# Head outputs turned on VectorE in 32x32 blocks, the blocks moved by DMA, and tokens kept in the turned order

## The chip, the cores and the metric

The kernel runs on one core of one Trainium2 chip. The metric is the device time of the core in microseconds. A core has TensorE (PE in the profile; its weight loads are PEld), VectorE (DVE), ScalarE (ACT), GpSimd (POOL) and SyncE (SP), each with an instruction queue of its own that runs in order. SP, ACT and POOL also issue DMAs.

## The reference

One encoder layer: 512 tokens, width 1024, all in float32. Two mixers work on the same normed input, their results are gated and summed, and a SwiGLU block follows.

```python
h = RMSNorm(x)
xc, gb, gc, q, k, v, g_sw, gate_a, gate_r = split(h @ W_in)

u    = gc * xc
conv = u[t-1] * w0 + u[t] * w1 + u[t+1] * w2
y_a  = (gb * conv) @ w_a_out

ret = retention(rotary(q), rotary(k), v)          # 4 heads, decayed in both directions
ret = (ret - mean(ret)) * rsqrt(var(ret) + eps) * g_ret     # per head and token
y_r = (ret * silu(g_sw)) @ w_r_out

x = x + (sigmoid(gate_a) * y_a + sigmoid(gate_r) * y_r) @ w_o
x = x + (silu(RMSNorm(x) @ w_gate) * (RMSNorm(x) @ w_up)) @ w_down
return RMSNorm(x)
```

A head has 256 query and key features and 512 value features.

## The kernel before

Every float32 product is made of three float32r matmuls (`mm3`): a number is split into a rounded part (hi) and the rest (lo), and hi x hi, hi x lo and lo x hi are added in PSUM. `split` makes the pair: ScalarE casts or scales the source into hi (L208, or L211 with a scale), VectorE subtracts it and stores lo (L209, or L212 with a scale). Many products use Strassen's scheme on quarters; the sums of weights which that needs are made on VectorE (L307).

Weights come from DRAM in units of 512 KB: SP loads a unit into one of ten raw tiles (L246 for plain blocks, L292 for quarters), and `split` makes its hi and lo tiles, of which there are five pairs. Large activations live in 14 "big" tiles of [128, 4, 512].

The part around the change runs over the four heads h. For each, `load_head` brings the scaled queries and keys, decay tables, values and swish gates from DRAM on SP (L879, L884). `do_pv` multiplies the scores with the values: four token tiles nb of 128 tokens, tokens on partitions and 512 features on the free axis; the mean and variance follow (L918 to L921), VectorE subtracts the mean and multiplies the gate (L927), ScalarE multiplies the reciprocal deviation (L929). The result lies in the gates' tile. The next head's scores follow (`do_scores`, `split_v`).

The projection `do_wr` needs the head output with features on partitions, so `do_t` turns it: `transpose` issues 16 VectorE instructions (L224), one for each pair (b, q) of a band of 32 partitions b and a quarter q of the features. Each reads 32 partitions x 512 elements in 32x32 blocks and writes them to band q of the target, so that tokens stand in natural order. Then four scaled splits (the gain `g_ret`) make the pair `yr`. `do_wr(h - 1)` runs next, while `do_t(h)` works: two halves of the 1024 output columns, each with 48 matmuls into four PSUM banks (`token_major`), then four evictions, which copy (L959) or add (L961) into `ysum`; with the last head they are also multiplied by the R gates `sgr` (L963). With head 0 the last convolution block `do_mix(3)` takes the place of `do_wr`. After the last head `do_wr(3)` runs directly behind `do_wr(2)`.

The convolution runs feature-major: `mix_quads` and `do_mix` make it in a tile c, multiply by the branch B in place (L870, L843), and `z_forms` splits the product and its Strassen sums and stores them to DRAM. `load_z` brings them back on POOL (L945), and the Strassen product that starts behind `do_wr(3)` reads them; its evictions (`merge`) multiply by the A gates `sga` and add `ysum`. After the output projection and the second norm the normed rows are transposed on TensorE. Until there the tokens of a tile nb are 128 nb + p on partition p.

In SwiGLU the same turning is done by `gated` (two transposes of 128x256 for a token tile, L1233) and `scatter` (16 DMAs on SP, L1243), which leave the tokens in another order: tile b, then j, then r for token 128 j + 32 b + r. The running sum is stored to DRAM in that order (L1335 to L1338), and the host puts the rows back at the end (L1529).

Tiles are placed and the instructions of each queue are put in order by a scheduler, mostly in the order of the program; `tc.issue_after(i)` puts the instructions of a block behind i on its engine.

Of the kernel before, what the change touches and what calls it, by code (L numbers as in the profile page):

```python
# [12 lines left out]
F32 = mybir.dt.float32  # L13
F32R = mybir.dt.float32r
AF = mybir.ActivationFunctionType
ALU = mybir.AluOpType

P = 128
D = 1024
S = 512  # L20
KD = D // P
NB = S // P
HEADS = 4
# [152 lines left out]
def block_kernel(ctx: ExitStack, tc: tile.TileContext, xw0, xw, xT, xtok, wpack, wquad, cols, decs, rot, g_ffn, g_final, out):  # L176
    nc = tc.nc
# [14 lines left out]
    def bigtile(dt=F32, n=4):  # L192
        return big.tile([P, n, 512], dt, tag="big", name="big", padded_shape=[P, 4, 512])
# [8 lines left out]
    low_of = [None]  # L202
    hi_of = [None]

    def split(src, hi, lo, scale=None, round=None):

        if scale is None:
            first = (round or nc.scalar.copy)(hi, src)  # L208
            low_of[0] = nc.vector.tensor_tensor(out=lo, in0=src, in1=hi.bitcast(F32), op=ALU.subtract)  # L209
        else:  # L210
            first = nc.scalar.activation(hi, src, AF.Copy, scale=scale)  # L211
            nc.vector.scalar_tensor_tensor(  # L212
                out=lo, in0=src, scalar=scale, in1=hi.bitcast(F32),
                op0=ALU.mult, op1=ALU.subtract)
        hi_of[0] = first
        return first

    def transpose(out, src):

        for b in range(4):  # L220
            for q in range(4):
                i = src[32 * b:32 * b + 32].rearrange("p j (i q c) -> p j i q c", q=4, c=32)
                o = out[32 * q:32 * q + 32].rearrange("p i (j b c) -> p j i b c", b=4, c=32)
                nc.vector.transpose(o[:, :, :, b, :], i[:, :, :, q, :])  # L224


    pos = [0]
    block = [0]
# [129 lines left out]
    def mm3(ps, left, right, first, last):  # L358
        (lh, ll), (rh, rl) = left, right
        nc.tensor.matmul(ps, lh, rh, start=first, stop=False)  # L360
        nc.tensor.matmul(ps, lh, rl, start=False, stop=False)  # L361
        nc.tensor.matmul(ps, ll, rh, start=False, stop=last)  # L362

    def act_pair(tiles, k, sl=slice(0, S)):
        hi, lo = tiles
        return hi[k // 4][:, k % 4, sl], lo[k // 4][:, k % 4, sl]
# [7 lines left out]
                mm3(ps, c.w(k, m * P, P), act_pair(rhs, k), k == 0, k == 7)  # L374
            evict(block0 + m, ps)

    def token_major(lhs, row0, chunks, evict, before=None):


        pss = [bank() for _ in range(NB)]  # L380
        n = 4 * chunks
        for kk in range(n):
            if kk % 4 == 0:
                c = Chunk()
            if before:
                before(kk)
            for nb in range(NB):
                mm3(pss[nb], act_pair(lhs, row0 + kk, slice(nb * P, (nb + 1) * P)),
                    c.w(kk % 4, 0, 512), kk == 0, kk == n - 1)
        for nb in range(NB):  # L390
            evict(nb, pss[nb])

# [117 lines left out]
    gret = cols_sb[:, O_GRET:O_GRET + 16]  # L510
# [134 lines left out]
    grd = [kept(f"gr{j}") for j in range(2)]  # L645
# [16 lines left out]
    for h in range(EARLY):  # L662
        pss = [bank() for _ in range(4)]
        for kk in range(8):
            if kk % 4 == 0:
                c = Chunk()
# [23 lines left out]
        t = bigtile()  # L690
# [138 lines left out]
        put(2, w)  # L829
        put(3, x2[:, 1:2])  # L830

    def do_mix(s):
        us, c = [], bigtile()[:, 0:2, :]
        feature_major(xg, lambda m, ps: us.append(snap(ps)))
        u = u_tile()

        def ev_c(m, ps):
            nc.vector.tensor_tensor(out=u[:, m, 1:513], in0=ps, in1=us[m], op=ALU.mult)
            conv(m, 2 * s + m, u[:, m], c[:, m])
        feature_major(xg, ev_c)  # L840

        def ev_b(m, ps):
            nc.vector.tensor_tensor(out=c[:, m], in0=ps, in1=c[:, m], op=ALU.mult)  # L843
        feature_major(xg, ev_b)
        z_forms(s, c)

    T1, T2 = slice(0, 256), slice(256, 512)

    def halves(t):
        return t.rearrange("p (m t) -> p m t", m=2)  # L850

    def mix_quads():

        c = bigtile().rearrange("p (s m) t -> p s m t", s=2)
        for s in range(2):
            u, got = u_tile(), {}

            def ev21(ps):
                nc.vector.tensor_tensor(out=u[:, :, 257:513], in0=halves(ps), in1=halves(got["c2"]), op=ALU.mult)

            def ev12(t):
                nc.vector.tensor_tensor(out=u[:, :, 1:257], in0=halves(got["x1"]), in1=halves(t), op=ALU.mult)
            fm_quad(xf, lambda t: got.update(x1=t), ev21, lambda t: got.update(c2=t), ev12)
            for m in range(2):
                conv(m, 2 * s + m, u[:, m], c[:, s, m])

        def times(s, t):
            def ev(b):
                o = c[:, s, :, t]
                nc.vector.tensor_tensor(out=o, in0=halves(b), in1=o, op=ALU.mult)  # L870
            return ev
        fm_quad(xf, times(0, T1), times(0, T2), times(1, T2), times(1, T1))
        for s in range(2):
            z_forms(s, c[:, s])


    def load(src, dt=F32):
        t = bigtile(dt)
        nc.sync.dma_start(t if dt == F32 else t.bitcast(F32), src)  # L879
        return t  # L880

    def load_head(h):
        tab = misctile(896, "tab")
        nc.sync.dma_start(tab, tabs[h])  # L884
        return [load(t, F32R) for t in qkd[h]], tab, load(vd[h]), load(sgd[h])

    def do_scores(qk, tab):
        p = (bigtile(F32R), bigtile(F32R))
# [40 lines left out]
            nc.scalar.activation(t, t, AF.Copy, scale=mv[:, 3:4])  # L929

    def do_t(h, t):
        tt = bigtile()
        transpose(tt, t)
        yr = (bigtile(F32R), bigtile(F32R))
        for eb in range(4):
            split(tt[:, eb, :], yr[0][:, eb, :], yr[1][:, eb, :], gret[:, 4 * h + eb:4 * h + eb + 1])
        return [yr[0]], [yr[1]]

    def load_z(groups):
        for j in groups:  # L940
# [7 lines left out]

    ysum, zf = [], {}

    def do_wr(h, yr):

        if h == 0:
            ysum.extend([bigtile(), bigtile()])
        for half in range(2):
            def ev(nb, ps):
                t = ysum[half][:, nb, :]
                if h == 0:
                    nc.scalar.copy(t, ps)  # L959
                else:  # L960
                    nc.vector.tensor_tensor(out=t, in0=ps, in1=t, op=ALU.add)  # L961
                if h == HEADS - 1:
                    nc.vector.tensor_tensor(out=t, in0=t, in1=sgr[half][:, nb, :], op=ALU.mult)  # L963
            token_major(yr, 0, 1, ev)

    mix_quads()
    nxt = load_head(0)
# [3 lines left out]
    yr = None  # L971
    for h in range(HEADS):
        if h < HEADS - 1:
            nxt = load_head(h + 1)
        else:
            load_z((0,))
        do_pv(p, vv, sg)
        t = sg
        if h < HEADS - 1:
            p = do_scores(nxt[0], nxt[1])  # L980
            vv, sg = split_v(nxt[2]), nxt[3]
        else:
            load_z((1, 2))
        new = do_t(h, t)
        if h == 0:
            do_mix(3)
        else:
            if h == HEADS - 1:
                sgr = [load(t) for t in grd]
            do_wr(h - 1, yr)  # L990
        yr = new


    load_z((3,))
    sga = [bigtile(), bigtile()]
    for t, d in zip(sga, gad):
        nc.gpsimd.dma_start(t, d)
    do_wr(HEADS - 1, yr)

    def merge(half, o):  # L1000
# [529 lines left out]
```

## Time and profile before

| | us |
|---|---|
| median of 3 runs | 1015.35 |
| lowest, highest | 1015.1, 1016.31 |
| the profiled execution | 1016.66 |
| its span | 1014.4 |
| PE busy in it | 1002.5 |
| DVE busy | 894.2 |
| ACT busy | 547.4 |
| POOL busy | 154.3 |
| mean granted clock of TensorE | 0.996 of full |

Times in the views are microseconds from the start of the span; where the page gives ns for one instruction, that is the mean. Matmuls overlap: one takes 0.39 us in the records, while the next starts after about 0.23. A line number names the line that issued the instruction, often a helper's. "x16" is the number of instructions in a row or group; what stands behind "<-" in brackets is the work that ended the idle time before it.

### The profile page before, as it was taken

The page shows a single profiled execution, that of the slowest core. Times are in us where ns is not written, and L with a number is a line of the kernel's source. Part 1 is how long each engine was busy: PE and PEld are TensorE (multiplying, and loading weights), DVE is VectorE, ACT ScalarE, POOL GpSimd, SP SyncE. Part 2 cuts the span into 40 slices and gives each one's busy share as a digit, 9 for nine tenths or more (in the row PEclk, how much of TensorE's full clock was granted, in tenths as well). Part 3 has the DMA queues.
Part 4 walks back from the last instruction along what each step waited for, and adds up shares of the span by engine and source line. Part 5 has one row for each costly group of instructions (what it writes and reads, how often), then busy time and mean ns, then how long its engine had stood idle before and what let it go on. Part 6 is the DMA issues. An engine that isn't in the chain of part 4 may idle for free.

```text
span 1014.4 us, 13342 instructions
## 1 busy us (share of the span) xinstructions
PE 1002.5 (99%) x4746; PEld 838.4 (83%) x4746; DVE 894.2 (88%) x1163; ACT 547.4 (54%) x736; POOL 154.3 (15%) x246
## 2 busy tenths in 40 slices
PE   9999999999999999999999999999999999999996
PEld 7888888888888998888888888888887888888884
DVE  7878898979798888697989997999988996989897
ACT  7547655553655455343452325577665555574664
POOL 0030221222122004112221200011101000003202
PEclk9999999999999999999999999999999999999998
DMA  9525587695767658839687865467677369486953
GB/s 352 189 76 184 185 289 219 206 306 177 231 191 257 222 217 276 332 131 331 154 306 257 288 233 180 127 202 231 167 228 152 139 208 267 107 248 127 274 140 104
DMA packets 60642, 215.87 MB, mean 213 GB/s; under 512 B 8928, under 2 KB 9056, under 8 KB 55968
## 3 DMA queue, kind: packets, MB, share of 16 engines
q1 hardware_dynamic: 42592, 144.73, 41.7%
q0 software_dynamic: 17696, 70.01, 25.6%
q8 instruction: 37, 0.61, 0.3%
q10 hardware_dynamic: 288, 0.29, 0.1%
q14 instruction: 29, 0.24, 0.1%
HBM read 171.21 MB, written 57.41 MB: 225 GB/s over the span
## 4 chain that ended last, share of the span: by engine, by line
PE 87%; DVE 8%; issue 2%; SPq 2%; DMA 1%; ACT 1%; POOL 0%; POOLq 0%; DVEq 0%; ACTq 0%
PE bank L445 48%; PE bank L360 10%; PE bank L361 10%; PE bank L362 10%; PE bank L401 8%; DVE wlo L209 2%; SPq L1243 2%; DVE raw L307 1%; DMA big<-turned 1%; DVE turned L1233 1%; DVE t L1229 1%; DVE t L1182 0%; DVE big L209 0%; PE bank L501 0%; ACT whi L208 0%
## 5 line engine op out<-in xcount | busy, mean ns | idle before, releaser
L208 ACT CAST whi<-raw 128x1024 fp32r<-128x1024 f32 (+2 forms) x299 | 301.8, 1028 | 239.0 <-PE bank L445 73.5
L209 DVE TENSOR_TENSOR wlo<-raw,whi 128x1024 fp32r<-128x1024 f32 (+2 forms) x300 | 350.8, 1189 | 69.6 <-ACT whi L208 68.9
L445 PE MATMUL bank<-whi,xform 128*128 128x512 f32 x1056 | 330.5, 390 | 0.0
L445 PEld LDWEIGHTS bank<-whi,xform 128*128 128x128 f32 x1056 | 198.0, 188 | 42.2 <-DVE xform L209 1.0
L445 PE MATMUL bank<-wlo,xform 128*128 128x512 f32 x528 | 205.8, 390 | 0.5 <-DVE wlo L209 0.5
L445 PE MATMUL bank<-whi,big 128*128 128x512 f32 x596 | 187.5, 390 | 0.3 <-ACT t L452 0.3
L307 DVE TENSOR_TENSOR raw<-raw 128x1024 f32<-128x1024 f32 x112 | 132.2, 1198 | 0.8
L445 PEld LDWEIGHTS bank<-whi,big 128*128 128x128 f32 x596 | 111.7, 188 | 24.5 <-ACT t L452 1.1
L445 PEld LDWEIGHTS bank<-wlo,xform 128*128 128x128 f32 x528 | 99.1, 188 | 22.1 <-DVE wlo L209 1.7
L445 PE MATMUL bank<-wlo,big 128*128 128x512 f32 x298 | 116.1, 390 | 0.1
L452 ACT COPY t<-bank 128x512 f32<-128x512 f32 x95 | 55.5, 587 | 70.8 <-PE bank L445 55.8
L360 PE MATMUL bank<-big,whi 128*128 128x512 f32 x220 | 85.7, 390 | 0.0
L362 PE MATMUL bank<-big,wlo 128*128 128x512 f32 x220 | 85.6, 389 | 0.0
L361 PE MATMUL bank<-big,whi 128*128 128x512 f32 x220 | 85.6, 389 | 0.0
L445 PEld LDWEIGHTS bank<-wlo,big 128*128 128x128 f32 x298 | 55.9, 188 | 12.0 <-DVE wlo L209 0.6
L401 PE MATMUL bank<-xform,whi 128*128 128x256 f32 x304 | 55.3, 283 | 0.2 <-ACT t L452 0.2
L360 PE MATMUL bank<-whi,big 128*128 128x512 f32 x128 | 49.8, 389 | 0.0
L361 PE MATMUL bank<-wlo,big 128*128 128x512 f32 x128 | 49.8, 389 | 0.0
L362 PE MATMUL bank<-whi,big 128*128 128x512 f32 x128 | 49.8, 389 | 0.0
L362 PEld LDWEIGHTS bank<-big,wlo 128*128 128x128 f32 x220 | 41.3, 188 | 8.7
L361 PEld LDWEIGHTS bank<-big,whi 128*128 128x128 f32 x220 | 41.3, 188 | 8.5
L360 PEld LDWEIGHTS bank<-big,whi 128*128 128x128 f32 x220 | 41.3, 188 | 8.5
(211 smaller groups left out, 1395.1 us busy)
## 6 DMA issues: line engine op xcount, KB each, us to landing
raw<-wquad SPq DMA_DIRECT2D x140, 512.0 KB, 5.2
raw<-wpack SPq DMA_DIRECT2D x42, 512.0 KB, 5.9
raw<-wquad POOLq DMA_DIRECT2D x16, 512.0 KB, 6.4
t_g<-wquad POOLq DMA_DIRECT2D x12, 512.0 KB, 7.7
z<-t POOLq DMA_DIRECT2D x24, 256.0 KB, 5.6
t_o<-wquad POOLq DMA_DIRECT2D x12, 512.0 KB, 6.7
zform<-z POOLq DMA_DIRECT2D x6, 1024.0 KB, 7.1
big<-turned SPq DMA_DIRECT2D x80, 64.0 KB, 4.5
```

Source lines behind the costliest of these rows:

```text
L208: first = (round or nc.scalar.copy)(hi, src)
L209: low_of[0] = nc.vector.tensor_tensor(out=lo, in0=src, in1=hi.bitcast(F32), op=ALU.subtract)
L307: nc.vector.tensor_tensor(out=t, in0=t, in1=raws[quad, more, u][:, 0:n], op=ALU.add)
L360: nc.tensor.matmul(ps, lh, rh, start=first, stop=False)
L361: nc.tensor.matmul(ps, lh, rl, start=False, stop=False)
L362: nc.tensor.matmul(ps, ll, rh, start=False, stop=last)
L401: nc.tensor.matmul(o, l[:, c], r[:, k], start=start and s == 0 and k == 0 and i == 0, stop=stop and k == 3 and i == 2, skip_group_check=True)
L445: nc.tensor.matmul(pss[tt], l, r[:, c], start=start and k == 0 and i == 0, stop=stop and k == n - 1 and i == 2, skip_group_check=True)
L452: nc.scalar.copy(t, ps)
L1229: nc.vector.tensor_tensor(out=s, in0=u, in1=s, op=ALU.mult)
L1233: nc.vector.transpose(t[:, :, :, j, :].rearrange("p q i r -> p i q r"), s.rearrange("p (i q c) -> p i q c", i=4, q=4)[:, :, 2 * h:2 * h + ...
L1243: nc.sync.dma_start(o[32 * q:32 * q + 32], turned[i][q // 2][32 * b:32 * b + 32, q % 2].rearrange("c i j r -> c (i j r)"))
```

## The change

`transpose` issues one VectorE instruction for each token tile, four a head, on all 128 partitions. Each turns the 32x32 blocks within their band of partitions and writes to a scratch tile t. Then 16 DMAs of 64 KB move band b, quarter q of t to band q of the target: on SP, for the last head alternately on SP and ACT. The tokens are thereby left in the turned order, as in SwiGLU.

The target is the lo tile of the pair `yr`; the splits are made in place from it (`split_t`), on strided views, and are issued later: behind the evictions of the first half of `do_wr(h - 1)`, with head 0 ahead of the last product of `do_mix(3)`.

What meets these tokens is arranged to the same order. The branch product of the convolution is written in turned order to a tile of its own (`z`) and, in `mix_quads`, by eight instructions of 256 elements in place of four of 512. The gates are loaded by four DMAs a tile (`load_turned`). The host lays out x in turned order. The running sum then needs no reordering on the host at the end. For the last head `load_z((1, 2))` is issued behind `do_t`.

```diff
-    def transpose(out, src):
+    def transpose(out, src, queues):
+        t = bigtile()
+        for j in range(NB):
+            o = t.rearrange("p q (i j r) -> p i q j r", i=4, j=4)[:, :, :, j, :]
+            nc.vector.transpose(o, src[:, j, :].rearrange("p (i q c) -> p i q c", i=4, q=4))
         for b in range(4):
             for q in range(4):
-                i = src[32 * b:32 * b + 32].rearrange("p j (i q c) -> p j i q c", q=4, c=32)
-                o = out[32 * q:32 * q + 32].rearrange("p i (j b c) -> p j i b c", b=4, c=32)
-                nc.vector.transpose(o[:, :, :, b, :], i[:, :, :, q, :])
+                queues[b % len(queues)].dma_start(out[32 * q:32 * q + 32, b, :], t[32 * b:32 * b + 32, q, :])
...
     def do_t(h, t):
-        tt = bigtile()
-        transpose(tt, t)
         yr = (bigtile(F32R), bigtile(F32R))
-        for eb in range(4):
-            split(tt[:, eb, :], yr[0][:, eb, :], yr[1][:, eb, :], gret[:, 4 * h + eb:4 * h + eb + 1])
-        return [yr[0]], [yr[1]]
+        transpose(yr[1].bitcast(F32), t, (nc.sync, nc.scalar) if h == HEADS - 1 else (nc.sync,))
+        return yr
+
+    def split_t(h, yr):
+        with tc.issue_after(hi_of[0].ins), tc.issue_after(low_of[0].ins):
+            for eb in range(4):
+                hi, lo = (x[:, :, P * eb:P * eb + P] for x in yr)
+                split(lo.bitcast(F32), hi, lo, gret[:, 4 * h + eb:4 * h + eb + 1])
...
-    def do_mix(s):
-        us, c = [], bigtile()[:, 0:2, :]
+    def do_mix(s, behind=None):
+        us, c = [], bigtile()
+        z = c[:, 2:4, :]
...
         def ev_b(m, ps):
-            nc.vector.tensor_tensor(out=c[:, m], in0=ps, in1=c[:, m], op=ALU.mult)
+            nc.vector.tensor_tensor(out=turned_order(z[:, m]), in0=by_token(ps), in1=by_token(c[:, m]), op=ALU.mult)
+        if behind:
+            behind()
         feature_major(xg, ev_b)
-        z_forms(s, c)
+        z_forms(s, z)
...
-        def times(s, t):
+        def times(s, half):
             def ev(b):
-                o = c[:, s, :, t]
-                nc.vector.tensor_tensor(out=o, in0=halves(b), in1=o, op=ALU.mult)
+                for m in range(2):
+                    t = slice(256 * half, 256 * half + 256)
+                    nc.vector.tensor_tensor(out=turned_order(z[:, s, m])[:, 2 * half:2 * half + 2], in0=by_token(halves(b)[:, m]),
+                                            in1=by_token(c[:, s, m, t]), op=ALU.mult)
...
+    def load_turned(queue, t, d):
+        for j in range(NB):
+            queue.dma_start(t[32 * j:32 * j + 32], d[:, j, :].rearrange("(m r) e -> r m e", m=4))
...
-    def do_wr(h, yr):
+    def do_wr(h, yr, behind=None):
...
-            token_major(yr, 0, 1, ev)
+            token_major(yr, ev)
+            if behind and not half:
+                behind()
...
-        else:
-            load_z((1, 2))
         new = do_t(h, t)
         if h == 0:
-            do_mix(3)
+            do_mix(3, lambda: split_t(0, new))
         else:
             if h == HEADS - 1:
-                sgr = [load(t) for t in grd]
-            do_wr(h - 1, yr)
+                load_z((1, 2))
+                sgr = [bigtile(), bigtile()]
+                for x, d in zip(sgr, grd):
+                    load_turned(nc.sync, x, d)
+            do_wr(h - 1, yr, lambda: split_t(h, new))
...
     for t, d in zip(sga, gad):
-        nc.gpsimd.dma_start(t, d)
+        load_turned(nc.gpsimd, t, d)
     do_wr(HEADS - 1, yr)
```

More of the change, by code (lines that the diff above doesn't have):

```diff
@@ L211, in split @@
             first = nc.scalar.activation(hi, src, AF.Copy, scale=scale)
-            nc.vector.scalar_tensor_tensor(
+            low_of[0] = nc.vector.scalar_tensor_tensor(
                 out=lo, in0=src, scalar=scale, in1=hi.bitcast(F32),
@@ L375, in feature_major, with token_major @@
             evict(block0 + m, ps)
-    def token_major(lhs, row0, chunks, evict, before=None):
+    def token_major(lhs, evict):
         pss = [bank() for _ in range(NB)]
[L381 to L386, printed above, removed]
+        c = Chunk()
+        for kk in range(4):
             for nb in range(NB):
-                mm3(pss[nb], act_pair(lhs, row0 + kk, slice(nb * P, (nb + 1) * P)),
-                    c.w(kk % 4, 0, 512), kk == 0, kk == n - 1)
+                mm3(pss[nb], tuple(x[:, nb, kk * P:(kk + 1) * P] for x in lhs), c.w(kk, 0, 512), kk == 0, kk == 3)
         for nb in range(NB):
@@ L830, in z_forms, with turned_order, by_token @@
         put(3, x2[:, 1:2])
-    def do_mix(s):
-        us, c = [], bigtile()[:, 0:2, :]
+    def turned_order(t):
+        return t.rearrange("p (b j r) -> p j b r", b=4, j=4)
+    def by_token(t):
+        return t.rearrange("p (j b r) -> p j b r", b=4, r=32)
+    def do_mix(s, behind=None):
+        us, c = [], bigtile()
+        z = c[:, 2:4, :]
         feature_major(xg, lambda m, ps: us.append(snap(ps)))
@@ L852, in mix_quads @@
     def mix_quads():
-        c = bigtile().rearrange("p (s m) t -> p s m t", s=2)
+        c, z = (bigtile().rearrange("p (s m) t -> p s m t", s=2) for _ in range(2))
         for s in range(2):
@@ L865, in mix_quads @@
                 conv(m, 2 * s + m, u[:, m], c[:, s, m])
-        def times(s, t):
+        def times(s, half):
             def ev(b):
-                o = c[:, s, :, t]
-                nc.vector.tensor_tensor(out=o, in0=halves(b), in1=o, op=ALU.mult)
+                for m in range(2):
+                    t = slice(256 * half, 256 * half + 256)
+                    nc.vector.tensor_tensor(out=turned_order(z[:, s, m])[:, 2 * half:2 * half + 2], in0=by_token(halves(b)[:, m]),
+                                            in1=by_token(c[:, s, m, t]), op=ALU.mult)
             return ev
-        fm_quad(xf, times(0, T1), times(0, T2), times(1, T2), times(1, T1))
+        fm_quad(xf, times(0, 0), times(0, 1), times(1, 1), times(1, 0))
         for s in range(2):
-            z_forms(s, c[:, s])
+            z_forms(s, z[:, s])
     def load(src, dt=F32):
@@ L1513 @@
         "xT": np.ascontiguousarray(xT[4:].transpose(1, 0, 2)),
-        "xtok": np.ascontiguousarray(a["x"][0].reshape(NB, P, D).transpose(1, 0, 2)),
+        "xtok": np.ascontiguousarray(a["x"][0].reshape(4, 4, 32, D).transpose(0, 2, 1, 3).reshape(P, NB, D)),
         "wpack": pack_weights(w),
@@ L1528 @@
     r = run_bass_kernel_spmd(nc, [arrays], core_ids=[0])
-    return r.results[0]["y"].reshape(4, 4, 32, D).transpose(1, 0, 2, 3).reshape(1, S, D)
+    return r.results[0]["y"].reshape(1, S, D)
```

## The prediction

> **What bounds the kernel now.** I read the page's busy shares first, then the view of waits for TensorE, then busy time by stage.
>
> ```profile
> PE 1002.5 (99%) x4746; PEld 838.4 (83%) x4746; DVE 894.2 (88%) x1163; ACT 547.4 (54%) x736; POOL 154.3 (15%) x246
> ```
>
> A busy share of 99% is not proof by itself, because the ends of matmuls are modelled. The waits of TensorE on all other engines are the better test (engine, line, releaser: us in total, times, longest):
>
> ```profile
> PE bank L501 <- DVE t L498: 1.4, 1, 1.4
> PE bank L445 <- DVE wlo L209: 0.5, 1, 0.5
> PE bank L445 <- ACT t L452: 0.3, 1, 0.3
> PE bank L401 <- ACT t L452: 0.2, 1, 0.2
> ```
>
> That is the whole list: 2.4 us, 1.4 of them at the first instruction. None comes from a line that the change touches. By stage (window, its length, then busy us and instructions of PE, PEld, DVE, ACT, POOL, then clock, DMA share, GB/s):
>
> ```profile
> 72.00:324.00 252.00, 252.00 (x1115) 208.53 (x1114) 217.60 (x237) 149.52 (x191) 54.98 (x98) 1.00 0.70 227
> 440.00:580.00 140.00, 140.00 (x619) 115.94 (x618) 127.22 (x199) 54.27 (x75) 23.83 (x38) 1.00 0.74 245
> 467.20:470.00 2.80, 2.80 (x14) 2.33 (x13) 0.00 (x0) 1.05 (x1) 0.00 (x0) 1.00 0.81 263
> 716.00:826.00 110.00, 109.15 (x479) 89.41 (x479) 101.72 (x129) 63.63 (x80) 7.08 (x8) 1.00 0.62 167
> 995.00:1014.40 19.40, 9.99 (x43) 7.62 (x41) 13.54 (x25) 9.06 (x22) 4.43 (x8) 0.81 0.29 109
> ```
>
> From 440 to 580, where the head outputs are made and turned, TensorE is busy for every microsecond at full clock, with VectorE at 127.22 of 140. Is a matmul there slowed by VectorE? Two starts inside a stretch in which VectorE does nothing, and two long runs from the chain that ended last:
>
> ```profile
> 467.37 0.39 PE L362 MATMUL bank<-big,wlo 128*128 128x512 f32 x1
> ...
> 470.09 0.39 PE L362 MATMUL bank<-big,wlo 128*128 128x512 f32 x1
> ```
> ```profile
> 73.24 152.47 PE bank L445 x672
> ...
> 825.32 130.03 PE bank L445 x570
> ```
>
> From 467.37 to 470.09 lie twelve matmuls (one each of L362, L360, L361 in turn): 2.72 / 12 = 0.2267 us each, with VectorE idle. The run from 73.24, with VectorE 217.60 / 252 = 86% busy, gives 152.47 / 672 = 0.2269. The pace does not depend on VectorE. So TensorE sets the time, and what VectorE saves is worth only what TensorE now waits for it: nothing between 440 and 580.
>
> **The change, part by part.** First the transposes (L224 now; L1233 is the same instruction on all 128 partitions in the later SwiGLU):
>
> ```profile
> L224 DVE STREAM_TRANSPOSE big<-big 32x512 f32<-32x512 f32 x64 | 45.0, 702 | 1.7 <-ACT big L929 0.9
> ...
> L1233 DVE STREAM_TRANSPOSE turned<-t 128x256 f32<-128x256 f32 x40 | 14.2, 409 | 0.0
> ```
>
> A head has 16 of 702 ns now and 4 of 128x512 afterwards. That form is not in the trace. If the price went by elements, 128x256 (twice those of 32x512) would cost 1.4 us; it costs 0.409. So it goes by the row length: 0.702 for 512, bounds 0.409 and 2.8. Sixteen of 0.702 are 11.2 us against 45.0: VectorE loses 33.8 us. On the path that is 0, since TensorE never waits there.
>
> Second, 64 DMAs of 64 KB on the SP queue, 16 a head. The same transfers exist in the later scatter (SP timeline, then the landing of that line's DMAs):
>
> ```profile
> 734.10 11.39 SPq L1243 DMA_DIRECT2D big<-turned  x16
> 745.58 7.57 SPq L292 DMA_DIRECT2D raw<-wquad  x8
> 766.96 15.39 SPq L1243 DMA_DIRECT2D big<-turned  x16
> ```
> ```profile
> DMA to landing us min/median/max: 1.9/4.5/7.6
> ```
>
> So 0.71 us of issue each (0.96 in the slow group), 11.4 to 15.4 us a head. What stands behind them on SP are the weight loads and the next head's loads. The last weight block of this part is loaded in the first row below, whose second DMA goes out at its end, 548.0, and is cast at 575.55 (ACT rows below): 27.5 us later. Take 15.4 off and 12.1 are left for a landing. SP itself stood for most of that 33.34 us waiting for a buffer, so the room is there. Price 0; with the cover gone, up to 15.4.
>
> ```profile
> 514.99 33.34 SPq L246 DMA_DIRECT2D raw<-wpack  x2
> ```
>
> Third, the last head, where only one projection lies between turning and use. ACT, VectorE and TensorE now:
>
> ```profile
> 560.84 0.72 ACT L929 ACTIVATE big<-big,bnmv 128x512 f32<-128x512 f32 x1 [1.27 <-POOL bnmv L921]
> 564.40 1.05 ACT L208 CAST whi<-raw 128x1024 fp32r<-128x1024 f32 x1 [2.84 <-PE bank L362]
> 569.84 1.05 ACT L208 CAST whi<-raw 128x1024 fp32r<-128x1024 f32 x1 [4.39 <-PE bank L362]
> 573.08 2.57 ACT L211 ACTIVATE big<-big,cols_sb 128x512 fp32r<-128x512 f32 x4 [2.19 <-DVE big L224]
> 575.55 1.04 ACT L208 CAST whi<-raw 128x1024 fp32r<-128x1024 f32 x1
> ```
> ```profile
> 561.60 11.45 DVE L224 STREAM_TRANSPOSE big<-big 32x512 f32<-32x512 f32 x16 [0.85 <-ACT big L929]
> 573.08 1.29 DVE L961 TENSOR_TENSOR big<-bank,big 128x512 f32<-128x512 f32 x2
> 574.28 2.73 DVE L212 SCALAR_TENSOR_TENSOR big<-big,cols_sb 128x512 fp32r<-128x512 f32 x4
> ```
> ```profile
> 580.48 0.39 PE L360 MATMUL bank<-whi,big 128*128 128x512 f32 x1
> ```
>
> The head output is complete at 560.84 + 0.72 = 561.56, and its projection begins on TensorE at 580.48. Now 16 transposes end at 573.05 and the first split pair (2.57 / 4 + 2.73 / 4 = 1.3 us) could be done at 574.4. Afterwards: four transposes to 561.6 + 2.8 = 564.4, eight DMAs on each of SP and ACT, 8 x 0.71 = 5.7 to 570.1, landing 4.5 to 574.6, first split pair to **575.9**: 4.6 us before TensorE asks. With the slow issue (7.7) and the longest landing (7.6) it is 581.0, 0.5 late. The later three pairs need 0.7 us each, while one step of the projection takes 12 x 0.2267 = 2.7, so they do not add. ACT's eight issues cost it 5.7 us in a stretch in which it casts two units and waits for TensorE. Price 0, bounds 0 and 0.5.
>
> The splits, now behind the first half of the previous projection, no longer stand ahead of its evictions (L961); they work in place, on strided views, at the same price: 0.
>
> Fourth, the small edits. Four products of the convolution (680 ns each, row below) become eight of half the width: between 0 and 2.7 us more on VectorE, where TensorE has no wait either. They are stored in runs of 32 elements; L1233 stores such runs too, at the price of its row length, so I add nothing. The products go to a tile of their own, one big buffer more until the z forms are made; a score product that waited for it has the next convolution's 144 matmuls (three weight blocks of 48, 144 x 0.2267 = 32.6 us) to hide behind. The gates come in four DMAs a tile instead of one, on SP and POOL; the R gates now land 6.9 us after issue. Room for them is made as soon as the head output is turned, and they are first read by the evictions of the projection that starts at 580.48, ten microseconds in. The z forms loaded behind the turning (7.1 us) are read only after that projection, 96 matmuls later: 580.48 + 96 x 0.2267 = 602.2. Price of all these 0.
>
> ```profile
> L870 DVE TENSOR_TENSOR big<-t,big x3: 676/680/683, 378.8 to 387.6; 128x512 f32<-128x512 f32 x3
> ```
> ```profile
> big<-gr SPq DMA_DIRECT2D x2, 1024.0 KB, 6.9
> ```
> ```profile
> zform<-z POOLq DMA_DIRECT2D x6, 1024.0 KB, 7.1
> ```
>
> **Sum: 0.** The profiled execution took 1016.66 us (span 1014.4, 2.3 around it), 1.3 above the median 1015.35. No change in it puts the median at **1015.3**. Its own range is 1014.3 to 1016.4, the spread of the runs shown.
>
> **The rivals.** *VectorE is the real bound (faster).* It is busier (88%) than TensorE's weight loads (83%); then its 33.8 us come off: 1015.35 - 33.8 = 981.5. Against it stand the wait list and the equal pace of 0.2267 with VectorE idle. Chance 0.02. The Trainium skill ("Perfetto Trace Analysis", Identifying the Most-Contended Engine) judges TensorE's headroom by the weight loads' busy share and not by matmul busy time, which by 83% against 88% would name VectorE. Here each matmul has one load, of 115.94 / 618 = 0.188 us in the row of 440 to 580, and 0.188 / 0.2267 is 83%: that is the share at full pace, and the trace goes against the rule.
>
> *Matmuls run faster beside less VectorE work.* If all of the pace above 512 columns' floor came from VectorE, 33.8 / 0.2267 = 149 matmuls would gain. The idle stretch bounds the gain at 0.2269 - 0.2267 a matmul: nothing. Chance 0.02. The Trainium skill ("TensorE: Matmul & The Clock Gate", Wait — 56ns, not 53.3ns?) gives 215.7 ns for 512 columns; as an estimate, 149 x 11 ns is 1.6 us, 1013.7. The trace shows no such pace anywhere quoted here.
>
> *The order behind the change shifts and the stalls of SwiGLU go (faster).* From 716 to 826: 110 - 479 x 0.2267 = 1.4 us. In the run from 825.32: 130.03 - 570 x 0.2267 = 0.8. Both gone: 1013.1. The change does not touch these lines. Chance 0.03.
>
> *The last head's blocks come late (slower).* It decides once they land after 580.5 - 1.3 = 579.2. If ACT's eight DMAs stand behind its cast of 569.84, which waits for TensorE, they begin at 570.9, land at 570.9 + 5.7 + 4.5 = 581.1, and TensorE loses 1.9 us (7.0 with slow issue and landing): 1017.2 to 1022.3. If SP's stand behind its loads that now wait until 579.37 (row below), it is 579.4 + 5.7 + 4.5 + 1.3 - 580.5 = 10.4: 1025.7. For it: both queues run in order, and SP waited 32 us at one load. Against it: the loads that wait so long are asked for later than the blocks are. Chance 0.15, of which 0.05 costs under 2 us.
>
> ```profile
> 573.11 4.30 SPq L879 DMA_DIRECT2D big<-gr  x2
> 579.37 4.99 SPq L292 DMA_DIRECT2D raw<-wquad  x3
> ```
>
> **How the numbers follow.** The forecast has 0.78. A measurement of this kernel tells about 0.2%, 2 us, from no change. Faster by more: 0.02 + 0.03 = 0.05. Slower by more: 0.10. Within: 0.78 + 0.02 + 0.05 = 0.85. The range runs from 1013.5, which takes in 1.8 of the 2.2 us of SwiGLU stalls, to 1018.0, which takes in the last head's delays up to 2.7 us; about 0.1 is left outside.
>
> **What would show it.** VectorE's busy time down to about 860 with TensorE's unchanged at 1002; four transposes of about 0.70 us a head; L211 of the last head starting near 574 and the matmul that now starts at 580.48 still there. I am wrong if TensorE shows a wait on L211, L212 or a DMA of turned blocks before 600, or if its busy time from 440 to 580 is under 140 us, or if the wait list was blind and the whole span shrinks with VectorE.

## The result and the profile after

| | before | after |
|---|---|---|
| median, us | 1015.23 (4 runs) | 1026.88 (4 runs) |
| lowest, highest | 1014.64, 1016.31 | 1025.94, 1029.62 |
| after / before | | 1.0118, 95% interval 1.0097 to 1.0139 |
| the profiled execution; its span | 1016.66; 1014.4 | 1025.94; 1024.2 |

The change costs 11.65 us by the medians, 9.8 by the spans of the two profiled executions. Line numbers below are those of the changed kernel: L361 to L363 are the matmuls of `mm3`, L223 the transposes, L226 the block DMAs, L211 and L212 the scaled splits, L308 the weight sums, L247 and L293 the weight loads, L885 the head loads, L896 the gates, L959 the z forms. First the busy line of the page, then TensorE's waits, all but 0.2 us for the first head's queries `qh` (engine, line, releaser: total, times, longest):

```profile
PE 1005.1 (98%) x4746; PEld 840.1 (82%) x4746; DVE 861.7 (84%) x1119; ACT 547.3 (53%) x736; POOL 158.1 (15%) x252
```
```profile
PE bank L361 <- ACT big L211: 4.3, 1, 4.3
PE bank L396 <- ACT t L447: 1.8, 2, 1.6
PE bank L496 <- DVE t L493: 1.4, 1, 1.4
PE bank L362 <- DMA big<-ql: 1.1, 1, 1.1
PE bank L363 <- DVE big L212: 1.0, 1, 1.0
```

VectorE lost 32.5 us of work, and TensorE gained waits in two places: at the last head's splits (L211, L212), which the change moved, and around the first head's scores (`ql`, and L396, the quad products beside them), whose lines it does not touch. By stage (window, length, busy us and instructions of PE, PEld, DVE, ACT, POOL, then clock, DMA share, GB/s):

```profile
440.00:580.00 140.00, 139.95 (x617) 115.56 (x617) 92.50 (x148) 53.49 (x75) 24.96 (x41) 1.00 0.78 245
583.20:588.00 4.80, 0.47 (x3) 0.06 (x1) 4.73 (x7) 1.88 (x3) 2.98 (x6) 1.00 1.01 346
588.00:596.00 8.00, 7.03 (x17) 5.21 (x18) 3.58 (x5) 1.73 (x3) 0.33 (x1) 0.57 1.02 381
```

From 440 to 580 TensorE is as busy as before, with VectorE at 92.50 in place of 127.22. Then come 5 us in which it stands, and 8 at little over half its clock. The matmuls there (TensorE's timeline of the changed kernel):

```profile
583.22 0.39 PE L363 MATMUL bank<-whi,big 128*128 128x512 f32 x1
587.94 0.50 PE L361 MATMUL bank<-whi,big 128*128 128x512 f32 x1 [4.33 <-ACT big L211]
588.27 0.40 PE L362 MATMUL bank<-wlo,big 128*128 128x512 f32 x1
589.64 0.79 PE L363 MATMUL bank<-whi,big 128*128 128x512 f32 x1 [0.97 <-DVE big L212]
590.23 0.63 PE L361 MATMUL bank<-whi,big 128*128 128x512 f32 x1
...
595.35 0.58 PE L361 MATMUL bank<-whi,big 128*128 128x512 f32 x1
595.77 0.40 PE L362 MATMUL bank<-wlo,big 128*128 128x512 f32 x1
```

From the start at 583.22 to that at 595.77 lie 17 matmuls. At the steady 0.2267 us they take 3.85; they took 12.55. **8.7 us are lost here**: about 5.6 in the two gaps, and 3.1 at the slow clock, where twelve steps from 590.23 to 595.35 take 0.427 us each. `do_wr(3)` itself was due at 583.22 + 0.23 = 583.45, against 580.48 before: **3.0 us were lost earlier**. Together 11.7, which is how much later SwiGLU's part begins (first matmul on a z form, before and after):

```profile
602.24 0.39 PE L445 MATMUL bank<-whi,zform 128*128 128x512 f32 x1
```
```profile
613.93 0.39 PE L440 MATMUL bank<-whi,zform 128*128 128x512 f32 x1
```

From there to the end of the span it is 412.2 us before and 410.3 after: 1.9 us come back, as some of SwiGLU's stalls are gone.

**The last head.** ACT, VectorE and SP of the changed kernel, to be read beside the rows of before in the prediction:

```profile
565.95 0.72 ACT L940 ACTIVATE big<-big,bnmv 128x512 f32<-128x512 f32 x1 [1.75 <-POOL bnmv L932]
567.45 10.76 ACTq L226 DMA_DIRECT2D big<-big  x8
...
583.70 1.05 ACT L208 CAST whi<-raw 128x1024 fp32r<-128x1024 f32 x1 [2.44 <-PE bank L363]
587.16 2.56 ACT L211 ACTIVATE big<-big,cols_sb 128x512 fp32r<-128x512 f32 x4 [2.42 <-DMA big<-big]
```
```profile
566.70 0.71 DVE L223 STREAM_TRANSPOSE big<-big 128x512 f32<-128x512 f32 x1 [0.85 <-ACT big L940]
...
586.44 2.48 DVE L308 TENSOR_TENSOR raw<-raw 128x1024 f32<-128x1024 f32 x2
588.84 2.73 DVE L212 SCALAR_TENSOR_TENSOR big<-big,cols_sb 128x512 fp32r<-128x512 f32 x4
```
```profile
449.01 10.33 SPq L226 DMA_DIRECT2D big<-big  x16
...
535.71 14.88 SPq L226 DMA_DIRECT2D big<-big  x16
...
567.48 10.47 SPq L226 DMA_DIRECT2D big<-big  x8
```

The head output is complete at 565.95 + 0.72 = 566.67, the last transpose ends at 567.41, and the last block lands near 587.1, where ACT's wait for it ends: 20 us on the way. The first head's blocks went out at 10.33 / 16 = 0.65 us each on SP alone; the last head's need 10.47 / 8 = 1.31 on each of two queues. What else moves then (the stretch of the first head's blocks and that of the last's, then the landing of L226's DMAs):

```profile
449.40:459.80 10.40, 10.40 (x48) 8.61 (x47) 3.30 (x4) 3.31 (x4) 0.00 (x0) 1.00 0.39 95
566.70:578.00 11.30, 11.30 (x51) 9.36 (x50) 3.44 (x5) 0.00 (x0) 3.97 (x7) 1.00 1.00 279
```
```profile
DMA to landing us min/median/max: 1.9/3.5/9.4
```

In the first, the 16 DMA engines are busy for 39% of the time; in the last, for all of it. The blocks are what L211 waits for last: 2.42 us in its row. But with the blocks in time the splits would not have run at once either. ACT's queue has four casts between its DMAs and L211: three right behind the DMAs, and the one of 583.70, which waited 2.44 us for TensorE to free a weight buffer and ends at 584.75. On VectorE, L212 stands behind two weight sums of together 2.48 us.

**The first head.** SP's timeline, before and after (the keys, `ql`, follow the queries within 0.5 us):

```profile
335.76 0.33 SPq L879 DMA_DIRECT2D big<-qh  x1
```
```profile
351.33 25.36 SPq L247 DMA_DIRECT2D raw<-wpack  x7
376.86 0.33 SPq L885 DMA_DIRECT2D big<-qh  x1
```

The head's queries and keys now go out 41 us later, behind seven weight loads. They land when TensorE already wants them: it waits for them at 385.5 and 387.3. The 1.6 us for L396, at 378, is a wait for ScalarE, and the experiments below show whether it belongs to this.

So there are two places, and at the last head two suspects in series: the blocks' DMAs, and the place of the splits in ACT's and VectorE's queues.

### The profile page after: what moved, and what is told of

Same layout as the page of the kernel before. It is cut to its first block, busy times and chain, and to the rows that moved or that the text cites. A ratio compares the mean times of both kernels' runs of the same rounds, so it can differ in the third digit from the quotient of the medians.

```text
span 1024.2 us, 13418 instructions
## 1 busy us (share of the span) xinstructions
PE 1005.1 (98%) x4746; PEld 840.1 (82%) x4746; DVE 861.7 (84%) x1119; ACT 547.3 (53%) x736; POOL 158.1 (15%) x252
## 4 chain that ended last, share of the span: by engine, by line
PE 67%; issue 16%; DVE 6%; DMA 5%; POOL 2%; SPq 1%; ACT 1%; ACTq 0%; POOLq 0%; DVEq 0%
PE bank L440 53%; PE bank L363 4%; PE bank L362 4%; PE bank L361 4%; PE bank L396 2%; DMA big<-big 2%; DMA z<-t 1%; DMA big<-ql 1%; POOL z L652 1%; SPq L226 1%; DVE wlo L209 1%; DMA gb<-g_ffn 1%; DVE big L938 1%; DVE big L209 1%; DVE bnst L929 1%
## 5 line engine op out<-in xcount | busy, mean ns | idle before, releaser
L308 DVE TENSOR_TENSOR raw<-raw 128x1024 f32<-128x1024 f32 x112 | 132.3, 1200 | 0.8
L361 PE MATMUL bank<-big,whi 128*128 128x512 f32 x220 | 85.7, 390 | 0.0
L363 PE MATMUL bank<-big,wlo 128*128 128x512 f32 x220 | 85.6, 389 | 0.0
L396 PE MATMUL bank<-xform,whi 128*128 128x256 f32 x304 | 55.3, 283 | 0.2 <-ACT t L447 0.2
L361 PE MATMUL bank<-whi,big 128*128 128x512 f32 x128 | 51.0, 399 | 4.3 <-ACT big L211 4.3
L363 PE MATMUL bank<-whi,big 128*128 128x512 f32 x128 | 51.2, 400 | 1.0 <-DVE big L212 1.0
L361 PEld LDWEIGHTS bank<-big,whi 128*128 128x128 f32 x220 | 41.3, 188 | 8.6
L363 PEld LDWEIGHTS bank<-big,wlo 128*128 128x128 f32 x220 | 41.3, 188 | 8.6
```

Source lines behind the costliest of these rows:

```text
L308: nc.vector.tensor_tensor(out=t, in0=t, in1=raws[quad, more, u][:, 0:n], op=ALU.add)
L396: nc.tensor.matmul(o, l[:, c], r[:, k], start=start and s == 0 and k == 0 and i == 0, stop=stop and k == 3 and i == 2, skip_group_check=True)
```

## The experiments

Each ratio is against the kernel before, timed beside it on the same chip.

### The z tile of `mix_quads` in raw buffers

The changed kernel, with the new tile `z` in two raw tiles in place of a big one.

```diff
-        c, z = (bigtile().rearrange("p (s m) t -> p s m t", s=2) for _ in range(2))
+        c = bigtile().rearrange("p (s m) t -> p s m t", s=2)
...
+        z = [rawtile().rearrange("p (m t) -> p m t", m=2) for _ in range(2)]
```

> The changed kernel with one edit: in mix_quads the turned products z go to two tiles of the weight staging pool instead of a big tile, so that no extra big tile is held. Theory 1 (the extra big tile puts off the first head's loads from 335.8 to 376.9, and the score products that filled TensorE's gaps between 377 and 390 come late): the loads go out near 335 again, TensorE's waits between 377 and 390 (1.7 + 0.35 + 1.3 us) go, and the span falls by 3.0 to 3.5 us to about 1021; the stall at 583 stays. Rival (the eight half-width products in turned order are what costs): the loads move but the span does not change by more than 0.5 us.

Measured: 1025.1 us (1023.71 to 1026.38), ratio 1.0088 (1.0073 to 1.0103). Queries and keys go out at 330.79, and the stalls between 377 and 390 are gone, that of L396 too. But the median falls by only 1.8 us, not 3.0 to 3.5, the intervals of the two ratios overlap, and the profiled span does not fall at all (1024.6 against 1024.2). At the last head TensorE arrives earlier and now waits 4.4 us for L211 and 3.2 for L212, where it was 4.3 and 1.0. The gain is given back at the next wait.

### The kernel before with that tile alone

```diff
-        c = bigtile().rearrange("p (s m) t -> p s m t", s=2)
+        c, z = (bigtile().rearrange("p (s m) t -> p s m t", s=2) for _ in range(2))
...
-                nc.vector.tensor_tensor(out=o, in0=halves(b), in1=o, op=ALU.mult)
+                nc.vector.tensor_tensor(out=z[:, s, :, t], in0=halves(b), in1=c[:, s, :, t], op=ALU.mult)
```

> The kernel before with one edit: in mix_quads the products go, in the old order and width, to a second big tile instead of in place. Theory 1: slower by 3.0 to 3.5 us, with the first head's loads near 377 and TensorE waits of the same size between 377 and 390. Rival (width and order of the products cost): within 0.5 us of the kernel before.

Measured: 1019.8 us (1019.03 to 1021.34) against 1016.05, ratio 1.0038 (1.0023 to 1.0053): 3.75 us for one tile, in a kernel that has nothing else of the change. Queries go out at 376.96, behind seven weight loads. TensorE's waits for the first head's loads in that run:

```profile
PE bank L360 <- DMA big<-qh: 1.6, 1, 1.6
PE bank L361 <- DMA big<-ql: 1.5, 1, 1.5
```

The first loss is shown from both sides: the tile takes one of the 14 big buffers, and the head's loads, which need such buffers, fall behind seven weight loads.

### The z forms ahead of the last head's turning

The changed kernel, with `load_z((1, 2))` issued ahead of `do_t(3)`, where the kernel before has it.

> The changed kernel with one edit: the loads of z form groups 1 and 2 (4 MB on POOL) are issued ahead of the last head's turning, as before the change. Theory 2 (they fill the DMA engines while the last head's blocks move; DMA share 1.00 from 566.7 to 578): the 8 + 8 block DMAs take 5 to 7 us instead of 10.5, the last block lands before 578, TensorE's waits on L211 and L212 (4.3 + 1.0 us) and the low clock behind them (about 3 us) go, and the span falls by 7 to 9 us. Rival a (the head's output itself is ready 5 us late, at 566.7, as VectorE interleaves the transposes with the statistics and makes head 2's splits first): the blocks still end within 2 us of 587, span at most 2 us shorter. Rival b (SP and ACT share one issuing rate of about 0.65 us a DMA): issue still takes 10.5 us, the last lands near 582, half of the stall stays.

Measured: 1030.49 us (1030.23 to 1030.71), ratio 1.0142 (1.0125 to 1.0159): 3.6 us slower than the changed kernel by the medians, not faster. From 560 to 577 the DMA share is 0.99 at 371 GB/s, the blocks go out in 13.50 us on SP and 12.82 on ACT (10.47 and 10.76 without the edit), and L211 starts at 591.30. The expectation was wrong: the last block lands later, not before 578. But most of that is no matter of how fast the DMAs run. On VectorE all four transposes now stand behind a weight split that waited for its cast:

```profile
567.50 1.23 DVE L209 TENSOR_TENSOR wlo<-raw,whi 128x1024 fp32r<-128x1024 f32 x1 [3.56 <-ACT whi L208]
568.64 2.49 DVE L223 STREAM_TRANSPOSE big<-big 128x512 f32<-128x512 f32 x4
```

They end at 571.13, where it was 567.41. From there to L211 it is 20.2 us, against 19.8 without the edit. So this run does not separate the loads from the order of the queues.

### All 16 blocks of the last head on SP

```diff
-        transpose(yr[1].bitcast(F32), t, (nc.sync, nc.scalar) if h == HEADS - 1 else (nc.sync,))
+        transpose(yr[1].bitcast(F32), t, (nc.sync,))
```

> The changed kernel with one edit: the last head's 16 block DMAs all go on SP. If the two queues share one rate, or the DMA engines' load sets it: 16 still take 10 to 12 us and the last block lands within 1.5 us of 587, the span is the same within 1.5 us. If each queue has its own pace under that load (1.3 us a DMA): 16 take about 21 us and the kernel is about 10 us slower.

Measured: 1027.91 us (1027.11 and 1028.7), ratio 1.0116 (1.0095 to 1.0136). SP needs 14.65 us for the 16, between the two values expected, where two queues needed 10.8: under load the second queue saves 4 us of issue, not half, and by the median nothing that can be told. The blocks land 4.6 us later (L211 starts at 591.79), and TensorE waits 8.2 us for L211 in place of 4.3. But L212 then follows without a wait, and fewer matmuls run at the slow pace behind the stop.

### The z forms behind the splits

```diff
-                load_z((1, 2))
...
-            do_wr(h - 1, yr, lambda: split_t(h, new))
+            do_wr(h - 1, yr, lambda: (split_t(h, new), load_z((1, 2)) if h == HEADS - 1 else None))
```

> The changed kernel, with the second and third pair of convolution forms loaded behind the last head's splits, not ahead of them; nothing else moved. Theory that the loads share the 16 DMA engines with the last head's 16 blocks and slow them: without the loads the blocks take 0.65 us each, as in the quiet stretch at 449 to 459 us (5.2 us if the two queues run side by side, 10.3 us if they share one rate), against 10.5 now; side by side they land near 574, and the whole loss at 583 to 596 us goes: 1017 to 1020 us. Rival, that the two queues share one rate whatever else runs: blocks still take over 9 us, landing near 578 to 580 after a start at 567.5, and with the splits the stall shrinks to 0 to 1 us. Rival, that the loads do not matter: L211's wait stays at over 3 us, 1025 us or more. New costs of the edit (forms not there when SwiGLU asks) would be seen as a wait on the z forms after 614 us.

Measured: 1021.8 us (1020.57 to 1023.85), ratio 1.0062 (1.0046 to 1.0078), between the two theories. The POOL timeline says why it tests little of the contention:

```profile
571.75 1.68 POOL L959 DMA_DIRECT2D zform<-z  x3
585.72 1.64 POOL L959 DMA_DIRECT2D zform<-z  x3 [12.29 <-DMA big<-big]
```

In the changed kernel one load went out at 566.86, three at 572.16 and two at 584.07; here one of them moved away from the blocks and the rest stayed. The blocks still take 9.38 us on SP and 11.16 on ACT. Two things came of it all the same. L211 starts 2.0 us earlier, at 585.18, and on VectorE L212 now stands ahead of the two weight sums (586.24 and 588.89), so that TensorE's only wait there is 2.5 us for L211. How the gain divides between the two, the run does not tell; the second points at the queues.

### The last head turned by VectorE, its splits left where they are

Sixteen instructions of 32x512 that write the turned order to a scratch tile; no block DMAs for this head.

```diff
+        if h == HEADS - 1:
+            tt = bigtile()
+            for b in range(4):
+                for q in range(4):
+                    i = t[32 * b:32 * b + 32].rearrange("p j (i q c) -> p j i q c", q=4, c=32)
+                    o = tt[32 * q:32 * q + 32, b, :].rearrange("p (i j r) -> p j i r", i=4, j=4)
+                    nc.vector.transpose(o, i[:, :, :, q, :])
...
```

> The changed kernel, with the last head alone turned as the kernel before did it: 16 VectorE instructions of 32 x 512 that write the turned order, no block DMAs for it (the other three heads keep one instruction a token tile and 16 DMAs on SP). Theory (the last head's blocks land late and TensorE waits for them): the head's output is complete near 566.7; 16 instructions of about 0.71 us are done near 578, the first split pair near 579.5, before TensorE asks at about 583.5; the stall of 4.3 us, the 1.0 us behind the two weight sums and the slow clock after them go, 7 to 9 us less: 1017.5 to 1020 us, with the 3.5 us of the extra tile left. Rival (what TensorE waits for there is VectorE's queue or something behind it): a wait of some us on the splits stays, over 1023 us.

Measured: 1024.99 us (1023.81 to 1026.81), ratio 1.0097 (1.0079 to 1.0115): 2 us, not 7 to 9. VectorE and ACT of that run:

```profile
563.52 11.46 DVE L951 STREAM_TRANSPOSE big<-big 32x512 f32<-32x512 f32 x16 [0.85 <-ACT big L940]
...
584.45 2.48 DVE L308 TENSOR_TENSOR raw<-raw 128x1024 f32<-128x1024 f32 x2
586.85 2.73 DVE L212 SCALAR_TENSOR_TENSOR big<-big,cols_sb 128x512 fp32r<-128x512 f32 x4
```
```profile
582.02 1.04 ACT L208 CAST whi<-raw 128x1024 fp32r<-128x1024 f32 x1 [4.40 <-PE bank L363]
582.97 2.56 ACT L211 ACTIVATE big<-big,cols_sb 128x512 fp32r<-128x512 f32 x4
```

The head is turned at 563.52 + 11.46 = 574.98, and its splits start 8 us later, behind a cast that had waited 4.40 us for a weight buffer; L212 stands behind the weight sums, three more. No DMA has a part in that. The theory with the blocks as the only cause falls.

### The same, with the z tile in raw buffers

> The changed kernel with both losses taken out: the last head turned by 16 VectorE instructions, and the z tile of the quad convolutions in two raw buffers in place of a big one. Theory (the two losses are all of the 11.6 us, and add): 3.4 and 8 to 9 us less, 1013.5 to 1017 us, level with the kernel before within 0.2%. Rival (the change also costs elsewhere, or the losses overlap): over 1019 us.

Measured: 1022.96 us (1021.95 to 1023.49), ratio 1.0070 (1.0054 to 1.0086). TensorE still waits 1.8 us for L211 and 3.1 for L212. The rival holds: something else was left.

### The place of the splits, with and without the blocks

Two kernels: the splits of the last head issued straight behind its turning, once with VectorE's turn and once with the block DMAs.

```diff
         new = do_t(h, t)
+        if h == HEADS - 1:
+            split_t(h, new)
...
-            do_wr(h - 1, yr, lambda: split_t(h, new))
+            do_wr(h - 1, yr, (lambda: split_t(h, new)) if h < HEADS - 1 else None)
```

> The run before last with one move more: the last head is turned by 16 VectorE instructions, and its splits are issued straight behind them, not behind the first half of the output product of the head before. Theory (two causes in series: the blocks' DMAs, and the splits' place in ACT's and VectorE's queues, behind a weight cast that waits 4.4 us for its buffer and two weight sums of 2.48 us; taking out one alone shows the other): the four splits run right after the turn, near 577 to 580 us, TensorE's two idle stretches (2 and 3.3 us) and the 16 matmuls at half pace (3.3 us) go: 1024 less 7 to 8.5 us, 1016 to 1018.5 us. Rival (the place of the splits costs nothing; VectorE is short of time here, 9.9 of 10 us busy at 570 to 580): the splits move, another VectorE instruction becomes late, TensorE still idles 4 us or more between 575 and 590: over 1021 us.

("The run before last" is the one with VectorE's turn and the splits left behind.)

> The changed kernel with its block DMAs kept, and only the last head's splits issued straight behind them, not behind the first half of the output product. Theory (two causes in series): the blocks still land near 584 to 587, so the splits now stand waiting at the head of ACT's and VectorE's queues, with weight casts and evictions behind them: no gain, 1025 to 1032 us, with TensorE's wait still on the splits or on a weight or a bank that stands behind them. Rival (the splits' place alone is the cause and the blocks are in time): 7 to 8.5 us less, 1018 to 1020 us.

Measured, as a square (median, ratio to before with its interval):

| | splits behind half of `do_wr(2)` | splits straight behind the turning |
|---|---|---|
| block DMAs | 1026.88, 1.0118 (1.0097 to 1.0139) | 1023.53, 1.0074 (1.0055 to 1.0092) |
| VectorE's turn | 1024.99, 1.0097 (1.0079 to 1.0115) | 1018.16, 1.0026 (1.0017 to 1.0036) |

With both taken out, the splits run as before the change (ACT, then VectorE):

```profile
577.38 2.57 ACT L211 ACTIVATE big<-big,cols_sb 128x512 fp32r<-128x512 f32 x4 [3.34 <-DVE big L951]
```
```profile
578.59 2.73 DVE L212 SCALAR_TENSOR_TENSOR big<-big,cols_sb 128x512 fp32r<-128x512 f32 x4
```

TensorE has no wait and no slow clock there. With the blocks kept, the splits stand early in the queue, and the blocks land as late as ever; the casts too come late, behind ACT's own DMAs:

```profile
568.10 13.15 ACTq L226 DMA_DIRECT2D big<-big  x8
581.34 2.00 ACT L208 CAST whi<-raw 128x1024 fp32r<-128x1024 f32 x2 [14.02 <-DMA big<-big]
587.82 2.56 ACT L211 ACTIVATE big<-big,cols_sb 128x512 fp32r<-128x512 f32 x4 [4.47 <-DMA big<-big]
```

Either edit alone gives 2 to 4 us (the 1.9 of VectorE's turn is not clear of noise by the intervals), both together about 9: two causes in series. The wait ends with the later of the two, so taking out one shows the other. That the early splits with the blocks gained 3.4 us by the median was not expected (no gain was); by the profiled spans it is 1.0, and what is lost there is still 4.7 us for L211.

### Both losses out, and the blocks with what helps them

> The run with VectorE's turn and early splits for the last head, and the z tile of the quad convolutions in raw buffers. Theory (these two places hold the whole loss): level with the kernel before or a little under it, since the SwiGLU part took 400.8 us after and 402.5 us before: 1013 to 1016.5 us. Rival (something of the change costs elsewhere): over 1018 us.

Measured: 1014.85 us (1013.13 to 1017.89, 10 runs) against 1015.78, ratio 0.9993 (0.9983 to 1.0003). That is level with the kernel before, 12 us under the changed one, and no faster than before within what can be told. The busy line of its page:

```profile
PE 1001.3 (99%) x4746; PEld 837.8 (83%) x4746; DVE 870.0 (86%) x1131; ACT 547.7 (54%) x736; POOL 155.4 (15%) x252
```

VectorE has 24 us less to do than in the kernel before, and the time is the same. The two places hold the whole loss.

> The changed kernel with all its block DMAs, the z forms loaded behind the last head's splits and the quad convolutions' z tile in raw buffers. Theory (the gains of the two edits add): 1021.8 less 2 to 3.5 us, 1018 to 1020 us, TensorE's wait at 580 to 586 us still there. Rival (the head start on TensorE makes the blocks later against it): 1021 us or more.

Measured: 1019.18 us (1017.21 to 1020.16), ratio 1.0028 (1.0018 to 1.0039), with TensorE's wait of 3.2 us for L211 still there. This is the best of the kernels that move all four heads' blocks by DMA.

### Two queues for every head

```diff
-        transpose(yr[1].bitcast(F32), t, (nc.sync, nc.scalar) if h == HEADS - 1 else (nc.sync,))
+        transpose(yr[1].bitcast(F32), t, (nc.sync, nc.scalar))
```

> The changed kernel with every head's 16 block DMAs on two queues, as the last head's are: 8 on SP, 8 on ACT. It is to measure how two queues stand to each other where little else moves: in the first head's stretch (449 to 460 us, DMA share 0.37) SP alone needed 10.33 us for 16 blocks. If each queue keeps its own pace, 8 + 8 blocks take 5.2 us there (0.65 us each) and the 10.5 us at the last head are the other loads' doing. If the blocks share one rate whatever the queue, they take near 10 us there (1.3 us each) and those loads are not needed to explain it. For the time of the whole kernel: ACT's casts stand behind its DMAs for three more heads, so no better than the changed kernel, 1026 to 1032 us.

Measured, in one run: 1035.41 us, with 1016.22 before. The blocks of the four heads on SP; ACT's eight are within 0.3 us of each:

```profile
450.15 5.43 SPq L226 DMA_DIRECT2D big<-big  x8
500.98 9.80 SPq L226 DMA_DIRECT2D big<-big  x8
538.80 13.58 SPq L226 DMA_DIRECT2D big<-big  x8
575.26 13.90 SPq L226 DMA_DIRECT2D big<-big  x8
```

That is more than the 1026 to 1032 expected; TensorE waits 10.1 us for L211 there. In the quiet stretch two queues halve the time: 8 + 8 blocks in 5.4 us, where SP alone needed 10.33. Each queue keeps its own pace. The same 8 + 8 take 13.6 to 13.9 us where other transfers fill the DMA engines (shares of 1.01 and 0.93 in the third and the last row). So the last head's 1.3 us a DMA is contention, and not a rate that belongs to the blocks. Which of the other transfers it is, no run separates. The Trainium skill ("DMA: Bandwidth & Descriptors", Issuing engines are not separate DMA queues) says that DMAs from any engine end on the same 16 DMA engines, and that a second issuing engine saves only the issue time. The loaded stretches agree; in the quiet one, at a DMA share of 0.63 over its 5.5 us, the issue time was all there was to save, and it halved.

## Why the prediction was wrong

**What held.** TensorE is the bound: 139.95 busy of 140 us from 440 to 580, though VectorE lost 32.5 us in all (33.8 predicted) and 24 us in the last repair, for nothing. A transpose on 128 partitions goes by its row length; the group's row after, with its mean:

```profile
L223 DVE STREAM_TRANSPOSE big<-big 128x512 f32<-128x512 f32 x16 | 10.3, 686 | 1.1 <-ACT big L940 1.1
```

That is 686 ns against 702 taken, near the lower part of the bounds 0.409 to 2.8. The block DMAs of the first three heads cost SP 10.3 to 14.9 us a head, against 11.4 to 15.4, and no weight came late for them: price 0. TensorE never waited for the z forms or the gates. The sign that was named for being wrong, a wait on L211 or L212 before 600, is what the trace shows.

**The third step, the last head, failed in four terms.** Priced 0, with bounds 0 and 0.5, it cost 8.7. *First*, the issue: 0.71 us each, from one queue alone and a DMA share of 0.71, where two queues at full share needed 1.31. The slow group, 0.96 at a share of 0.93, served only for the bound; it was a hint that the price of a DMA depends on its company. *Second*, the landing: 4.5, at the longest 7.6, by a line in another part of the kernel; it was 9.4 at the longest here. *Third*, the start: transposes and issue were set behind 561.56, the old completion. It came at 566.67. TensorE's loss at the first head accounts for 3.0 of these 5.1 us (with the z tile in raw buffers the output was complete at 563.74); the rest goes with VectorE, where the transposes now stand among the statistics. With that tile in raw buffers too, and the head turned by VectorE behind the statistics, it is complete at 561.12, though head 2's splits still wait for their own blocks. *Fourth*, and hidden behind the blocks: "could be done" one split pair after landing. The new place of the splits was read only as a relief (they no longer stand ahead of the evictions). What stands ahead of *them* now was not asked: a cast that waits for TensorE, and two weight sums. The cast is there by the kernel's own order, as `split_t` is issued behind the last weight split (`tc.issue_after`). The row of before at 569.84, with its 4.39 us of waiting for TensorE, was in the prediction.

**The price of being late was also short.** The rival of the late blocks counted the wait itself, 1.9 to 10.4 us. It did not count that TensorE goes on at half pace after standing: 3.1 us on top of 5.6.

**The fourth step, the extra big tile, failed.** The prediction gave it 32.6 us of cover, and asked what a score product would wait for. But it looked at the products and not at the loads ahead of them: queries and keys need big buffers of their own, and on SP they fell behind seven weight loads, 41 us. It cost 3.75 us alone, 0 predicted.

**The z forms and the gates** were priced at their old landings, 7.1 and 6.9 us. After the change (landing in the last column):

```profile
zform<-z POOLq DMA_DIRECT2D x6, 1024.0 KB, 13.7
...
big<-gr SPq DMA_DIRECT2D x8, 256.0 KB, 20.3
```

As waits they cost nothing, as predicted. As traffic they were not priced at all: the z forms now go out at 566.86 and 572.16, beside the blocks, where the kernel before had sent four of them by 559. What they alone cost the blocks is not shown, as the two kernels that moved them changed the order of VectorE too.

**The rivals.** "The last head's blocks come late" was the right one, with chance 0.15 and up to 1025.7 us. Its two sources were wrong: ACT's DMAs went out at 567.45 and did not stand behind a cast, and SP's not behind blocked loads. It happened through contention and through the splits' place. VectorE as the bound and a quicker pace of the matmuls did not show; of SwiGLU's stalls, worth 2.2 us there at most, some went, and the part is 1.9 us shorter.

## What to carry to other kernels

The price of a DMA belongs to the stretch in which it runs: take issue and landing from a stretch with the same DMA share and as many queues, and where the share goes to 1, let the one result that TensorE waits for not depend on a DMA. When work is moved behind other work, list what stands ahead of it in each in-order queue, for every queue that it uses; when a tile is added to a full pool, follow the next loads that need a slot. And where one repair gives less than the wait that it should remove, look for a second cause behind it before dropping the first: here each alone gave 2 to 4 us and both about 9.

## What was not expected of the hardware

TensorE's clock after a short stop is not settled by the length of the stop. Two runs (window, length, busy of PE, PEld, DVE, ACT, POOL, clock, DMA share, GB/s): the z forms behind the splits, after an idle time of 2.54 us, and the same with the z tile in raw buffers, after 3.22:

```profile
586.00:591.00 5.00, 5.00 (x16) 3.96 (x17) 4.97 (x7) 1.74 (x3) 3.53 (x7) 0.69 1.02 306
```
```profile
583.60:589.00 5.40, 5.21 (x22) 3.95 (x23) 5.37 (x7) 1.76 (x3) 3.54 (x7) 1.00 1.06 306
```

The shorter stop was followed by a clock of 0.69, the longer by full speed. After the two stops of the changed kernel, 4.33 and 0.97 us, it was 0.57 over 8 us. The Trainium skill ("TensorE: Matmul & The Clock Gate", What's actually happening) describes a free-running window of about 3.4 us, with an array that is throttled to half after an idle window and released after a busy one. A stop of 3.22 us without a slow clock agrees with that. The slow clock behind 2.54 us, less than one window, does not, unless a window that is only mostly idle counts, which no run here shows. The 0.427 us a step measured here is the pace at half clock for 512 columns that the same page gives, 426.7 ns (section "Wait — 56ns, not 53.3ns?"). A stop of 2.5 us or more may so cost more than itself: 1.6 us at the slow pace behind 2.54, 1.7 behind the 8.2 of the kernel with all 16 blocks on SP, 3.1 behind the two stops of the changed kernel, and next to nothing behind 3.22.
